# Thirty-two experts as a fixed pipeline on TensorE, with the 32-row experts in 256 columns

## The chip, the cores and the metric

One core of a Trainium2 chip (trn2) runs the whole program. The metric is device time in microseconds of one execution. Before the change it is 2638.91 us, the median of three runs (2637.82 to 2639.2).

## The reference, cut to what matters

The program computes two transformer blocks on 512 tokens of width 1024. Only the last part matters here: the mixture of experts at the end of the second block, and the final norm.

```python
def hierarchical_moe(h, w_rg, b_rg, w_re, b_re, w1, w3, w2):
    ...
    comb = g_w[:, None] * top_p / jnp.sum(top_p, axis=-1, keepdims=True)
    expert = g_idx[:, None] * EXPERTS_PER_GROUP + top_i.astype(jnp.int32)
    ...
    def run_block(args):
        x_blk, e = args
        return (jax.nn.silu(x_blk @ w1[e]) * (x_blk @ w3[e])) @ w2[e]
    ...
    yb = yb * buf_w[:, None].astype(yb.dtype)
    out = jnp.zeros((n_tok + 1, d), yb.dtype).at[buf_tok].add(yb)[:n_tok]
```

Each token goes to two of 32 experts. An expert has two first matrices (w1 and w3, 1024 x 512 each) and a second one (w2, 512 x 1024), all float32: 6 MB in all. The rows that the experts return are weighted, added to their tokens, and the sum is normalised.

## The kernel before, in words

The expert stage is `phase_d`. A router sorts the experts by the number of their tokens; the expert of rank r gets `CAPS[r]` rows: 64, 128 (two experts) or 32 (the last twelve). `GROUPS` puts them into groups of 128 rows (two experts of 64, four of 32, one of 128), and `SEQ` is the order of the 32 experts through the groups: two groups of 64-row experts, four 32-row experts, a 128-row one, two groups of 64, four of 32, a 128-row one, five groups of 64, and four 32-row experts at the end. A few tokens beyond the capacities would go through a loop behind the stage.

Weights come in loads of 1024 KB from SP's queue (`Experts.steps`, L1743): four tiles `w31` per expert (each two of the eight steps of the contraction, w3 and w1 side by side) and two tiles `w2`. All share 18 buffers, three experts' worth, in three pools; a load is issued when a buffer has been read for the last time.

For one group, `begin` selects the group's rows on VectorE (`select`, L1784, into the single buffer `f_sel`), TensorE gathers the rows and turns them (`rows`, L1793), VectorE scales them into `f_X` (L1847), and small products give each row's weight (L1856). For one expert, `hidden` makes the first products: for 64 rows (L1894), p3 and p1 stand in the two halves of one PSUM bank, so that each product uses half the columns of the array and two run beside each other; for 32 rows (L1880), four parts of 128 columns stand beside each other in the array, in two banks. SiLU on ScalarE and a product on VectorE follow (L1896, L1897; L1883, L1884), then `turn_hidden` transposes on TensorE (L1905), ScalarE copies (L66), and `project` makes the second products (L1936; for 32 rows `project_half`, L1918), which `K.split` takes from PSUM into a high and a low half, ScalarE first (L71) and VectorE second (L72). When a group is done, `turned` transposes its selection (L1868), and `scatter` adds the group's rows to the tokens in eight steps (two products each, L1944, and an addition on VectorE, L1946). `last_rows` and `finish` do the last expert, the last scatter, the norm and the stores.

The order on each engine is not that of the text: a planner takes what is ready by its own costs. `issue_after` keeps scatter, turned selection and the next group's rows behind the first products of the current expert; everything else mixes.

Of the kernel before, what the change touches and what calls it, by code (L numbers as in the profile page):

```python
# [10 lines left out]
F32 = mybir.dt.float32  # L11
# [5 lines left out]
AF = mybir.ActivationFunctionType  # L17
OP = mybir.AluOpType
# [1729 lines left out]
def phase_d(K, out):  # L1748
# [3 lines left out]
    with ExitStack() as st:  # L1752
# [90 lines left out]
        def gather(n, sel, combs, room):  # L1843

            X = wk.tile([128, 8, 128], F32, name="f_X", bufs=1)
            for hf, ps in enumerate(room):
                V.tensor_tensor(X[:, 4 * hf:4 * hf + 4, :n], ps[:, :, :n],  # L1847
                                gc[:, 4 * hf:4 * hf + 4, None].to_broadcast([128, 4, n]), op=OP.mult)
            c = wk.tile([128, 4], F32, name="f_c")
            pt = tps.tile([128, 4, 128], F32, name="f_t")  # L1850
            m = n // len(combs)
            top = 128 if m == 32 else m
            for i, w in enumerate(combs):
                for p in range(0, top, m):
# [14 lines left out]
            K.copy(selT[:n], pt[:n], 1)  # L1869
            return selT  # L1870

        def hidden(ts, M, X, c):
            g = wk.tile([128, 512], F32, name="f_g", bufs=1)
            if M == 32:
                p3, p1 = [hps.tile([128, 512], F32, name="f_hp")[:, 0:128] for _ in range(2)]
                for k in range(8):
                    for w, p in enumerate((p3, p1)):
                        for j in range(4):
                            c0 = k % 2 * 1024 + w * 512 + j * 128
                            last = PE.matmul(p[32 * j:32 * j + 32], X[:, k], ts["w31", k // 2][:, c0:c0 + 128],  # L1880
                                             start=k == 0, stop=k == 7, skip_group_check=True,
                                             tile_position=(0, 32 * j))
                S.activation(g[:, 0:128], p1, AF.Silu)  # L1883
                V.scalar_tensor_tensor(g[:, 0:128], p3, c, g[:, 0:128], op0=OP.mult, op1=OP.mult)  # L1884
                return g, last
            if M == 64:
                ps = hps.tile([128, 512], F32, name="f_hp")
                p3, p1 = ps[0:64], ps[64:128]
            else:
                p3, p1 = [hps.tile([128, 512], F32, name="f_hp")[:] for _ in range(2)]  # L1890
            for k in range(8):
                for w, p in enumerate((p3, p1)):
                    c0 = k % 2 * 1024 + w * 512
                    last = PE.matmul(p, X[:, k], ts["w31", k // 2][:, c0:c0 + 512], start=k == 0, stop=k == 7,  # L1894
                                     skip_group_check=True)
            S.activation(g[:M], p1, AF.Silu)  # L1896
            V.scalar_tensor_tensor(g[:M], p3, c[:M], g[:M], op0=OP.mult, op1=OP.mult)  # L1897
            return g, last

        def turn_hidden(M, h):  # L1900

            pg = tps.tile([128, 4, 128], F32, name="f_t")
            n, m = (1, 128) if M == 32 else (4, M)
            for q in range(n):
                PE.transpose(pg[:, q, :m], h[:m, q * 128:(q + 1) * 128], K.ident[:m, :m])  # L1905
            gT = wk.tile([128, 4, 128], F32, name="f_gT", bufs=1)
            K.copy(gT[:, :n, :m], pg[:, :n, :m], 1)
            if M == 32:
                return [gT[:, 0, 32 * q:32 * q + 32] for q in range(4)]
            return [gT[:, q, :M] for q in range(4)]  # L1910

        def project_half(ts, gT, y, a, hf):

            ps = [xps.tile([128, 512], F32, name="f_xp") if hf else yps.tile([128, 512], F32, name="f_yp") for _ in range(2)]
            for k in range(4):
                for j in range(4):
                    c0 = k * 512 + j * 128
                    PE.matmul(ps[j % 2][32 * j:32 * j + 32, 0:128], gT[k], ts["w2", hf][:, c0:c0 + 128],  # L1918
                              start=k == 0, stop=k == 3, skip_group_check=True, tile_position=(0, 32 * j))
            for j in range(4):  # L1920
                cs = slice(128 * j, 128 * j + 128)
                K.split(ps[j % 2][32 * j:32 * j + 32, 0:128], y[0][a:a + 32, hf, cs], y[1][a:a + 32, hf, cs])

        def project(ts, M, gT, y, a):

            if M == 32:
                for hf in range(2):
                    project_half(ts, gT, y, a, hf)
# [19 lines left out]
        def scatter(n, selT, y):  # L1948
            for b in range(NB):
                for hf in range(2):  # L1950
                    add_rows(n, selT, y, b, hf, (yps if hf else xps).tile([128, 512], F32, name="f_yp" if hf else "f_xp"))

        def last_rows(ts, gT, selT, y, a):

# [25 lines left out]
        def finish(parts):  # L1980
# [16 lines left out]
            for b in range(NB):  # L1997
                y = ys[b // 2][:, b % 2]
                V.scalar_tensor_tensor(y, K.x[:, b], rstd[:, b:b + 1], gf, op0=OP.mult, op1=OP.mult)  # L1999
                nc.sync.dma_start(out[b * 128:(b + 1) * 128, :], y)  # L2000

        nxt = begin(0)
        n = 0
        done = None
        for g, rs in enumerate(GROUPS):
            X, sel, c = nxt
            y = None
            for i, r in enumerate(rs):
                M = CAPS[r]
                if n < len(loaded):  # L2010
                    ts = loaded[n]
                elif n < NFIX:
                    ts = W.load(r)
                else:
                    ts = W.load(regs[r])
                    index(n + AHEAD)
                if n == NFIX - 1:
                    for q in range(NFIX, NFIX + AHEAD):
                        index(q)
                h, last = hidden(ts, M, X[:, :, M * i:M * i + M], c[:, i:i + 1])  # L2020
                if n == 0:
                    R.ranks(order, byrank)
                    R.thirds(ranked, byrank[:, 1])
                if i == 0:
                    with tc.issue_after(last.ins):
                        if done:
                            scatter(*done)
                        selT = turned(128, sel)
                if i == len(rs) - 1 and g + 1 < len(GROUPS):
                    with tc.issue_after(last.ins):  # L2030
                        nxt = begin(g + 1)
                gT = turn_hidden(M, h)
                if i == 0:
                    y = halves()
                if n < 31:
                    project(ts, M, gT, y, M * i)
                if n == NFIX:
                    with tc.issue_after(last.ins):
                        R.tables(tab, nov, tabd)
                n += 1  # L2040
            done = 128, selT, y
        finish(last_rows(ts, gT, selT, y, M * i))

        n_over = nc.values_load(nov[0:1, 0:1], min_val=0, max_val=NOV)  # L2044
        nc.sync.dma_start(rankd[:], byrank[:].rearrange("p a b r -> p (a b) r"))
        with tc.For_i(0, n_over, 1) as i:  # L2046
# [16 lines left out]
            project(ts, 64, turn_hidden(64, hidden(ts, 64, X[:, :, :64], c[:, 0:1])[0]), y, 0)  # L2063
            scatter(64, turned(64, sel), y)
            finish(iter(()))


# [315 lines left out]
```

## Time and profile before

| | |
|---|---|
| median of three runs | 2638.91 us |
| the profiled execution | 2639.42 us, span 2637.6 us |
| TensorE products, share of the span | 2491.0 us, 94% |
| VectorE, ScalarE | 1784.1 us (68%), 919.6 us (35%) |
| expert stage | first product at 2136.35 us, last second product ends at 2613.41 us |
| weights of the experts | 192 loads of 1024 KB |

The shares are averages over stages with different limits. The stage before the experts is not touched, so only the last 500 us are read. PE is TensorE, DVE is VectorE, ACT is ScalarE, SPq is the queue of SP. One float32 product is two records on PE. A time in brackets after a row is idle time of the engine before it, with what ended it.

### The profile page before, as it was taken

How to read it: one execution, taken by the hardware profiler on the slowest of the kernel's cores; microseconds unless marked ns; L12 is line 12 of the kernel's file. 1: busy time of each engine (PE TensorE's matmuls, PEld its weight loads, DVE VectorE, ACT ScalarE, POOL GpSimd, SP SyncE). 2: the span in 40 equal slices, each digit the busy share in tenths (PEclk: the TensorE clock that was granted, in tenths of full speed). 3: DMA queues.
4: the chain of work that ended last, by engine and by line, in shares of the span. 5: the costliest groups of instructions: out<-in, count | busy, mean ns of one | idle time of the engine just before them, and what ended most of it. 6: DMA issues, size and time to landing. Idle time of an engine off the chain costs nothing. (4 is left out here: it accounts for less than half of the span.)

```text
span 2637.6 us, 43720 instructions
## 1 busy us (share of the span) xinstructions
PE 2491.0 (94%) x17112; PEld 2075.5 (79%) x17112; DVE 1784.1 (68%) x3778; ACT 919.6 (35%) x1607; POOL 379.6 (14%) x261
## 2 busy tenths in 40 slices
PE   6999999999879999999999998999999989989995
PEld 5887988998869999999998787888797856565554
DVE  6654789988847777878888997576753673333334
ACT  4532533455533333333333344343532412121112
POOL 0000000000004555545555420000000000000000
PEclk8999999999989999999999998898999999999998
DMA  6237122338868999998998973222133489999995
GB/s 244 73 115 241 57 92 81 112 118 253 244 237 300 328 323 322 330 325 314 328 327 322 353 269 117 80 81 72 62 115 116 179 328 401 409 404 386 400 390 213
DMA packets 183483, 623.92 MB, mean 237 GB/s; under 512 B 15846, under 2 KB 66406, under 8 KB 156650
## 3 DMA queue, kind: packets, MB, share of 16 engines
q1 hardware_dynamic: 146410, 486.87, 49.6%
q0 software_dynamic: 36864, 134.23, 14.6%
q8 instruction: 135, 2.21, 0.3%
q14 instruction: 74, 0.61, 0.1%
HBM read 591.55 MB, written 29.49 MB: 235 GB/s over the span
## 5 line engine op out<-in xcount | busy, mean ns | idle before, releaser
L72 DVE TENSOR_TENSOR w_lo<-w_raw,w_hi 128x1024 fp32r<-128x1024 f32 x228 | 278.2, 1220 | 250.1 <-ACT w_hi L71 247.0
L71 ACT CAST w_hi<-w_raw 128x1024 fp32r<-128x1024 f32 x228 | 238.5, 1046 | 579.5 <-issue 205.6
L78 PE MATMUL b_ups<-hT,w_lo 128*128 128x384 f32 x1024 | 347.3, 339 | 6.7 <-DVE w_lo L72 6.5
L76 PE MATMUL b_ups<-hT,w_hi 128*128 128x384 f32 x1024 | 349.6, 341 | 1.4 <-ACT x_sb L919 1.0
L77 PE MATMUL b_ups<-hT,w_hi 128*128 128x384 f32 x1024 | 346.2, 338 | 0.0
L942 POOL DMA_INDIRECT x_sb<-in_u_rows,b_eg x128 | 191.9, 1499 | 979.9 <-ACT b_wh L71 741.2
L76 PE MATMUL b_acc<-b_vh,b_wh 128*128 128x512 f32 x756 | 295.7, 392 | 17.7 <-ACT b_vh L71 17.7
L77 PE MATMUL b_acc<-b_vl,b_wh 128*128 128x512 f32 x756 | 296.7, 392 | 2.9 <-DVE b_vl L72 2.7
L78 PE MATMUL b_acc<-b_vh,b_wl 128*128 128x512 f32 x756 | 295.9, 391 | 0.0
L76 PE MATMUL p_acc<-w_hi,hT 128*128 128x256 f32 x896 | 256.4, 286 | 3.0 <-ACT hT L71 2.8
L77 PE MATMUL p_acc<-w_lo,hT 128*128 128x256 f32 x896 | 253.5, 283 | 1.4 <-DVE w_lo L72 1.3
L78 PE MATMUL p_acc<-w_hi,hT 128*128 128x256 f32 x896 | 253.1, 283 | 0.3 <-DVE hT L72 0.3
L942 POOL DMA_INDIRECT x_sb<-in_v,b_eg x128 | 187.4, 1464 | 199.6 <-DVE b_accg L959 167.0
L78 PEld LDWEIGHTS b_ups<-hT,w_lo 128*128 128x128 f32 x1024 | 194.2, 190 | 9.0 <-DVE w_lo L72 8.9
L76 PEld LDWEIGHTS b_ups<-hT,w_hi 128*128 128x128 f32 x1024 | 194.6, 190 | 6.6 <-ACT b_a L919 1.7
L77 PEld LDWEIGHTS b_ups<-hT,w_hi 128*128 128x128 f32 x1024 | 194.3, 190 | 3.0
L76 PEld LDWEIGHTS p_acc<-w_hi,hT 128*128 128x128 f32 x896 | 171.3, 191 | 18.8 <-issue 13.2
L76 PEld LDWEIGHTS b_acc<-b_vh,b_wh 128*128 128x128 f32 x756 | 142.8, 189 | 44.9 <-ACT b_vh L71 17.9
L77 PEld LDWEIGHTS p_acc<-w_lo,hT 128*128 128x128 f32 x896 | 172.0, 192 | 2.2 <-DVE w_lo L72 1.8
L1894 PE MATMUL f_hp<-f_w,f_X 128*64 128x512 f32 (+1 forms) x640 | 171.4, 594 | 0.7 <-DVE f_X L1847 0.6
L78 PEld LDWEIGHTS p_acc<-w_hi,hT 128*128 128x128 f32 x896 | 170.7, 191 | 1.4 <-DVE hT L72 0.8
L71 ACT CAST b_wh<-b_wfull 128x384 fp32r<-128x384 f32 x128 | 65.4, 514 | 298.8 <-PE b_acc L77 276.4
(660 smaller groups left out, 4916.2 us busy)
## 6 DMA issues: line engine op xcount, KB each, us to landing
f_w<-in_w SPq DMA_DIRECT2D x192, 1024.0 KB
w_raw<-in_u SPq DMA_DIRECT2D x128, 512.0 KB
b_vraw<-in_v SPq DMA_DIRECT2D x128, 512.0 KB
b_gd<-g_sg SPq DMA_DIRECT2D x12, 2048.0 KB
b_g<-b_gd SPq DMA_DIRECT2D x32, 768.0 KB
a_ar_t<-in_w_ada SPq DMA_DIRECT2D x32, 512.0 KB
w_raw<-in_w_tok SPq DMA_DIRECT2D x20, 512.0 KB
a_ar_t<-in_w_ada SPq DMA_DIRECT2D x8, 1024.0 KB
```

The lines of the kernel that those rows point to most:

```text
L71: self.nc.scalar.copy(hi, src)
L72: self.nc.vector.tensor_tensor(lo, src, hi, op=OP.subtract)
L76: first = mm(ps, a[0], b[0], start=start, stop=False)
L77: mm(ps, a[0], b[1], start=False, stop=False)
L78: mm(ps, a[1], b[0], start=False, stop=stop)
L942: nc.gpsimd.indirect_dma_start(out=r, out_offset=None, in_=d[src], in_offset=bass.IndirectOffsetOnAxis(ap=eg[:, k:k + 1], axis=0))
L1894: last = PE.matmul(p, X[:, k], ts["w31", k // 2][:, c0:c0 + 512], start=k == 0, stop=k == 7, skip_group_check=True)
```

## The change

`hidden` gets a function `between` that is called after each of the first seven steps of the contraction. `plan` fills it: in the first expert of a group of several it holds the transposes of the expert before; in the second also the scatter of the former group, two steps at a time, and the turned selection; a group's only expert takes all of it, with the former expert's second products. After an expert's first products (and, for the last expert of a group, the rows of the next group) come the second products of the expert before. A context `in_order` fixes TensorE's order to the order of the text for the whole loop; the `issue_after` blocks go. The 32-row experts have 256 columns per part in place of 128: one PSUM bank for the first products, one for the second, half the instructions, two transposes in place of one. For 128 rows one of the two PSUM banks of the first products comes from the pool `f_xp`.

```diff
-            top = 128 if m == 32 else m
+            top = max(m, 64)
...
-        def hidden(ts, M, X, c):
+        def hidden(ts, M, X, c, between=None):
+
             g = wk.tile([128, 512], F32, name="f_g", bufs=1)
+            ps = hps.tile([128, 512], F32, name="f_hp")
             if M == 32:
-                p3, p1 = [hps.tile([128, 512], F32, name="f_hp")[:, 0:128] for _ in range(2)]
-                for k in range(8):
...
+                n, m = 64, 256
             else:
-                p3, p1 = [hps.tile([128, 512], F32, name="f_hp")[:] for _ in range(2)]
+                n, m = M, 512
+            if M == 128:
+                parts = [(ps, 0, 0, None), (xps.tile([128, 512], F32, name="f_xp"), 1, 0, None)]
+                p3, p1 = parts[0][0][:], parts[1][0][:]
+            else:
+                p3, p1 = ps[0:64, :m], ps[64:128, :m]
+                parts = [(p3, 0, 0, None), (p1, 1, 0, None)]
+                if M == 32:
+                    parts = [(ps[q:q + 32, :m], q // 64, q % 64 // 32 * m, (0, q)) for q in range(0, 128, 32)]
             for k in range(8):
...
+                if between and k < 7:
+                    between(k)
...
-            n, m = (1, 128) if M == 32 else (4, M)
+            n, m = (2, 64) if M == 32 else (4, M)
...
-        def project_half(ts, gT, y, a, hf):
...
+            if M == 32:
+                ps = yps.tile([128, 512], F32, name="f_yp")
+                for k in range(4):
+                    for j in range(4):
+                        c0 = k * 512 + j % 2 * 256
+                        PE.matmul(ps[32 * j:32 * j + 32, 0:256], gT[k], ts["w2", j // 2][:, c0:c0 + 256],
+                                  start=k == 0, stop=k == 3, skip_group_check=True, tile_position=(0, 32 * j))
                 for j in range(4):
...
+                    cs = slice(j % 2 * 256, j % 2 * 256 + 256)
+                    K.split(ps[32 * j:32 * j + 32, 0:256], y[0][a:a + 32, j // 2, cs], y[1][a:a + 32, j // 2, cs])
...
+        def plan(rw, M, first, second, sel):
+
+            p = {}
+            at = lambda k, *f: p.setdefault(k, []).extend(f)
+            if first and second:
+                at(0, rw.turn)
+                at(1, rw.project, lambda: rw.leave())
+                for k in (3, 4, 5, 6):
+                    at(k, rw.scatter_two)
+                at(6, lambda: rw.turned(sel))
+            else:
+                at(3 if M == 64 else 4, rw.turn)
+                if second:
+                    for k in ((2, 3, 4, 5) if M == 64 else (4, 5, 6, 6)):
+                        at(k, rw.scatter_two)
+                    at(5 if M == 64 else 6, lambda: rw.turned(sel))
+            return lambda k: [f() for f in p.get(k, ())]
...
+        with in_order(tc, ("PE",)):
+            for g, rs in enumerate(GROUPS):
...
+                    alone = len(rs) == 1
+                    h = hidden(ts, M, X[:, :, M * i:M * i + M], c[:, i:i + 1], plan(rw, M, i == 0, i == 1 or alone, sel))
...
+                    if i == len(rs) - 1 and g + 1 < len(GROUPS):
                         nxt = begin(g + 1)
...
+                    if not alone:
+                        rw.project()
+                        if i == 0:
+                            rw.leave()
+                    rw.before = ts, M, M * i, h
```

## Rows read from the trace of the kernel before

**Rows 1.** DMA view, 2140 to 2600 us: all transfers of the stretch.

```profile
DMA packets 25156, 183.32 MB, mean 399 GB/s; under 512 B 2783, under 2 KB 2783, under 8 KB 2845
```

**Rows 2.** Busy time by stretch: us of each engine, then clock, DMA share, GB/s.

```profile
2140.00:2200.00 60.00, 59.48 (x518) 30.95 (x518) 35.21 (x80) 10.97 (x19) 0.00 (x0) 1.00 0.96 387
2200.00:2275.00 75.00, 66.53 (x930) 45.49 (x924) 26.65 (x66) 13.83 (x46) 0.00 (x0) 0.98 1.01 418
2275.00:2337.00 62.00, 61.12 (x436) 35.63 (x432) 21.28 (x40) 8.53 (x16) 0.00 (x0) 1.00 0.98 398
...
2413.00:2578.00 165.00, 162.69 (x1054) 88.37 (x1056) 56.27 (x102) 24.45 (x46) 0.00 (x0) 1.00 0.96 386
2578.00:2602.00 24.00, 19.04 (x507) 16.76 (x503) 11.49 (x28) 6.64 (x23) 0.00 (x0) 1.00 0.95 384
```

**Rows 3.** Waits of SP and TensorE in the expert stage: us, times, longest.

```profile
SPq L1743 <- PE f_yp L1936: 176.5, 26, 15.2
SPq L1743 <- PE f_hp L1894: 78.0, 63, 14.5
...
PEld f_hp L1894 <- DMA f_w<-in_w: 0.5, 2, 0.2
```

**Rows 4.** TensorE in order of time, one group of two 64-row experts: start, us.

```profile
2512.76 7.04 PE L1894 MATMUL f_hp<-f_w,f_X 128*64 128x512 f32 x32
2519.72 0.73 PE L1944 MATMUL f_xp<-f_y,f_selT 128*128 128x512 f32 x2
...
2522.13 0.40 PE L1868 MATMUL f_t<-f_id,f_sel 128*128 128x128 f16 x4
...
2524.92 3.94 PE L1936 MATMUL f_yp<-f_w,f_gT 128*64 128x512 f32 x14
...
2536.52 3.75 PE L1793 MATMUL f_xp<-f_sel,f_hs 128*128 128x128 f16 x64
...
2540.55 0.46 PE L1905 MATMUL f_t<-f_ident,f_g 64*128 64x64 f32 x4
2541.52 3.65 PE L1936 MATMUL f_yp<-f_w,f_gT 128*64 128x512 f32 x16 [0.52 <-ACT f_gT L66]
2545.01 1.46 PE L1894 MATMUL f_hp<-f_w,f_X 128*64 128x512 f32 x6
```

**Rows 5.** TensorE in order of time: one first product, two scatter steps, first products.

```profile
2175.95 1.07 PE L1894 MATMUL f_hp<-f_w,f_X 128*64 128x512 f32 x2
2176.95 0.74 PE L1944 MATMUL f_xp<-f_y,f_selT 128*128 128x512 f32 x2
...
2178.10 1.08 PE L1894 MATMUL f_hp<-f_w,f_X 128*64 128x512 f32 x4
```

**Rows 6.** TensorE in order of time, 32-row experts, second and last group of four.

```profile
2337.42 3.70 PE L1880 MATMUL f_hp<-f_w,f_X 128*32 128x128 f32 x128
...
2361.34 1.58 PE L1880 MATMUL f_hp<-f_w,f_X 128*32 128x128 f32 x49 [2.51 <-issue]
...
2381.18 14.00 PE L1894 MATMUL f_hp<-f_w,f_X 128*128 128x512 f32 x32
...
2601.05 1.94 PE L1880 MATMUL f_hp<-f_w,f_X 128*32 128x128 f32 x59 [2.99 <-issue]
...
2611.45 1.08 PE L1918 MATMUL f_yp<-f_w,f_gT 128*32 128x128 f32 x32 [0.41 <-ACT f_gT L66]
2612.35 1.06 PE L1918 MATMUL f_xp<-f_w,f_gT 128*32 128x128 f32 x32
```

**Rows 7.** VectorE in order of time, the same 64-row group: selections and product.

```profile
2525.94 0.75 DVE L1784 TENSOR_TENSOR f_sel<-f_cd,f_byrank 128x256 f16<-128x256 f32 x2
...
2537.25 0.74 DVE L1897 SCALAR_TENSOR_TENSOR f_g<-f_hp,f_c,f_g 64x512 f32<-64x512 f32 x1 [6.19 <-ACT f_g L1896]
```

**Rows 8.** Groups by line and shape: VectorE, low halves of 32-row second products.

```profile
L72 DVE TENSOR_TENSOR f_y<-f_xp,f_y 32x128 fp32r<-32x128 f32 x48 | 13.8, 287 | 3.5 <-ACT f_y L71 2.0
```

More of the change, by code (lines that the diff above doesn't have):

```diff
@@ L1870, in turned @@
             return selT
-        def hidden(ts, M, X, c):
+        def hidden(ts, M, X, c, between=None):
             g = wk.tile([128, 512], F32, name="f_g", bufs=1)
+            ps = hps.tile([128, 512], F32, name="f_hp")
             if M == 32:
-                p3, p1 = [hps.tile([128, 512], F32, name="f_hp")[:, 0:128] for _ in range(2)]
-                for k in range(8):
[L1877 to L1888, printed above, removed]
-            else:
-                p3, p1 = [hps.tile([128, 512], F32, name="f_hp")[:] for _ in range(2)]
-            for k in range(8):
[L1892 to L1898, printed above, removed]
@@ new lines, in hidden @@
+            for k in range(8):
+                for p, w, c0, at in parts:
+                    c0 += k % 2 * 1024 + w * 512
+                    PE.matmul(p if M < 128 else p[:], X[:, k], ts["w31", k // 2][:, c0:c0 + m], start=k == 0, stop=k == 7,
+                              skip_group_check=True, **({"tile_position": at} if at else {}))
+                if between and k < 7:
+                    between(k)
+            S.activation(g[:n, :m], p1, AF.Silu)
+            V.scalar_tensor_tensor(g[:n, :m], p3, c[:n], g[:n, :m], op0=OP.mult, op1=OP.mult)
@@ L1900, in turn_hidden @@
+            return g
         def turn_hidden(M, h):
             pg = tps.tile([128, 4, 128], F32, name="f_t")
-            n, m = (1, 128) if M == 32 else (4, M)
+            n, m = (2, 64) if M == 32 else (4, M)
             for q in range(n):
@@ L1908, in turn_hidden @@
             if M == 32:
-                return [gT[:, 0, 32 * q:32 * q + 32] for q in range(4)]
+                return [gT[:, q % 2, q // 2 * 32:q // 2 * 32 + 32] for q in range(4)]
             return [gT[:, q, :M] for q in range(4)]
-        def project_half(ts, gT, y, a, hf):
[L1914 to L1922, printed above, removed]
         def project(ts, M, gT, y, a):
             if M == 32:
-                for hf in range(2):
-                    project_half(ts, gT, y, a, hf)
+                ps = yps.tile([128, 512], F32, name="f_yp")
[4 more added lines that the diff above has]
+                                  start=k == 0, stop=k == 3, skip_group_check=True, tile_position=(0, 32 * j))
+                for j in range(4):
+                    cs = slice(j % 2 * 256, j % 2 * 256 + 256)
+                    K.split(ps[32 * j:32 * j + 32, 0:256], y[0][a:a + 32, j // 2, cs], y[1][a:a + 32, j // 2, cs])
                 return
@@ L1946, in add_rows, with scattering @@
             V.tensor_tensor(x, x, ps[:], op=OP.add)
-        def scatter(n, selT, y):
+        def scattering(n, selT, y):
             for b in range(NB):
@@ L1951, in scatter @@
                     add_rows(n, selT, y, b, hf, (yps if hf else xps).tile([128, 512], F32, name="f_yp" if hf else "f_xp"))
+                    yield
         def last_rows(ts, gT, selT, y, a):
@@ L2000, in finish, with turn, project, scatter_two @@
                 nc.sync.dma_start(out[b * 128:(b + 1) * 128, :], y)
+        class Rows:
+            before = None
+            scatter = None
+            selT = y = done = None
+            def turn(self):
+                if self.before:
+                    self.gT = turn_hidden(self.before[1], self.before[3])
+            def project(self):
+                if self.before:
+                    ts, M, a, _ = self.before
+                    if not a:
+                        self.y = halves()
+                    project(ts, M, self.gT, self.y, a)
+            def scatter_two(self):
+                if self.scatter:
+                    for _ in range(2):
+                        next(self.scatter, None)
+            def turned(self, sel):
+                self.selT = turned(128, sel)
@@ L2002, in phase_d, with leave @@
+        rw = Rows()
+        def leave():
+            rw.scatter = scattering(128, rw.selT, rw.y) if rw.y else None
+        rw.leave = leave
         nxt = begin(0)
         n = 0
[L2004 to L2030, printed above, removed]
-                        nxt = begin(g + 1)
[L2032 to L2038, printed above, removed]
@@ new lines, in phase_d @@
+        with in_order(tc, ("PE",)):
+            for g, rs in enumerate(GROUPS):
+                X, sel, c = nxt
+                for i, r in enumerate(rs):
+                    M = CAPS[r]
+                    if n < len(loaded):
+                        ts = loaded[n]
+                    elif n < NFIX:
+                        ts = W.load(r)
+                    else:
+                        ts = W.load(regs[r])
+                        index(n + AHEAD)
+                    if n == NFIX - 1:
+                        for q in range(NFIX, NFIX + AHEAD):
+                            index(q)
+                    alone = len(rs) == 1
+                    h = hidden(ts, M, X[:, :, M * i:M * i + M], c[:, i:i + 1], plan(rw, M, i == 0, i == 1 or alone, sel))
+                    if n == 0:
+                        R.ranks(order, byrank)
+                        R.thirds(ranked, byrank[:, 1])
+                    if i == len(rs) - 1 and g + 1 < len(GROUPS):
+                        nxt = begin(g + 1)
+                    if not alone:
[3 more added lines that the diff above has]
+                    rw.before = ts, M, M * i, h
+                    if n == NFIX:
@@ L2039, in phase_d @@
                         R.tables(tab, nov, tabd)
-                n += 1
-            done = 128, selT, y
-        finish(last_rows(ts, gT, selT, y, M * i))
+                    n += 1
+        ts, M, a, h = rw.before
+        gT, y, selT = turn_hidden(M, h), rw.y, rw.selT
+        finish(last_rows(ts, gT, selT, y, a))
         n_over = nc.values_load(nov[0:1, 0:1], min_val=0, max_val=NOV)
@@ L2062, in phase_d @@
             y = halves()
-            project(ts, 64, turn_hidden(64, hidden(ts, 64, X[:, :, :64], c[:, 0:1])[0]), y, 0)
-            scatter(64, turned(64, sel), y)
+            project(ts, 64, turn_hidden(64, hidden(ts, 64, X[:, :, :64], c[:, 0:1])), y, 0)
+            for _ in scattering(64, turned(64, sel), y):
+                pass
             finish(iter(()))
```

## The prediction

> **What bounds the kernel now.** I read the profile from the whole to the single product. The change touches only the expert stage, from the first product at 2136 us to the end at 2637.6 us. I cut that stage into stretches and looked at the DMA column first [rows 2]: the transfers move 384 to 418 GB/s in every stretch, while TensorE's busy column is nearly full too. Two resources are close to their limit, so the next question is which one waits for the other.
>
> The stage's weight transfers say how far the DMA side is from full. From 2140 to 2600 us 183.3 MB move at a mean of 399 GB/s [rows 1]; the best long stretch, 2200 to 2275, holds 418 GB/s with a share of 1.01 [rows 2]. I take 418 as full. Against it the stretches lost: 2140 to 2200, 60 x (1 - 387/418) = 4.4 us; 2275 to 2337, 62 x (1 - 398/418) = 3.0 us; 2413 to 2578, 165 x (1 - 386/418) = 12.6 us. That is 20.0 us in which transfers had nothing to do. The last stretch, 24 us at 384, holds 22.0 us of full rate, so the last weights land near 2600.
>
> The waits name the cause [rows 3]: SP, which issues the loads, waits 176.5 us for second products (L1936) and 78.0 us for first products (L1894) to free a buffer, while TensorE waits for a load 0.5 us in all. So TensorE is the pacer where the queue runs dry, and the queue where it does not.
>
> A group of two 64-row experts shows the pacer [rows 4]: 2512.76 to 2545.01, 32.25 us. One load of 1024 KB at 418 GB/s takes 2.51 us, six per expert, so two experts need 30.1 us of transfer: 2.15 us of dry queue per group, and five such groups (10.8 us) make most of the 12.6. Four 32-row experts are the reverse [rows 6]: TensorE is through in 43.8 us (2337.42 to 2381.18), their loads need 60.2 us, and the buffers filled ahead are used up.
>
> **The change, part by part.** *64-row group on TensorE.* Its pieces today, start to start [rows 4]: first products 6.96 us; second products 3.49; rows and weights of the next group 4.03 (2536.52 to 2540.55); transposes 0.46; the turned selection 0.40. The second stretch of products, 2524.92 to 2536.52, takes 11.60 where 6.96 + 3.49 = 10.45 would do, because products of two experts are mixed there; with the gap of 0.52 us before 2541.52 and the slow end of the scatter that is what a fixed order can give back. New: the scatter goes in four pairs between first products. An interrupted pair took 1.15 us (2176.95 to 2178.10) [rows 5], five uninterrupted steps (2519.72 to 2522.13, four of the five rows left out) 2.41 us, or 0.96 a pair [rows 4]. I take 1.15, since the new pairs are interrupted. Sum: 2 x 6.96 + 2 x 3.49 + 4.03 + 2 x 0.46 + 0.40 + 4 x 1.15 = 30.85 us, 1.40 less than now and still 0.75 above the transfers' 30.1. With 0.96 it is 30.1.
>
> *The waits on the way.* The transposes now stand four steps (3.5 us) after the former expert's products end; SiLU and the product on VectorE must fit in, and 0.74 us for the latter [rows 7] leaves room. The new wait to watch is the selection: its buffer is single, it is read until the turned selection after step five, and the next group's rows follow after two more steps, 2 x 0.87 = 1.74 us. Behind it on VectorE stand two scatter additions; two selections took 0.75 us in all [rows 7]. That fits if they run before the product of the expert just finished, as today (2525.94 against 2537.25). If they come behind it, the rows wait for SiLU, product and selections: the product ended at 2537.99, 1.47 us after the first products gave way to the rows at 2536.52 [rows 4, 7], and 0.75 comes on top, 2.2 us per group; TensorE's whole order is then held, since it is fixed. I take 0, with 2.2 as the upper end.
>
> *32-row experts.* Twice the columns, half the instructions, same streamed columns: the 3.70 us of one expert's first products [rows 6] stay. The exposed chain before each expert's transpose and second products, and the unexplained gaps of 2.51 and 2.99 us [rows 6], go or shrink; one transpose becomes two (0.46 / 4 = 0.12 us more). Evacuation: eight parts of 287 ns become four [rows 8], bounded by 4 x 287 and 4 x 574 ns, off the path. TensorE gains about 10 us per group of four, but the 60.2 us of loads set this stretch: worth nothing by itself. What it does is keep the buffers emptier when the 64-row groups begin.
>
> *128-row experts* lose the pause in which nothing but scatter ran; loads bind there, I count nothing. Halved weight products beside the rows: hidden by the same pacing.
>
> *Late release.* The second weights of an expert are now freed after the next expert's first products (6.96 us later) and, for the first of a pair, after the next rows too (4.03 us). Loads behind them on SP's list wait along. At the start, where every buffer is full and TensorE paces, this costs between 0 and 11 us of dry queue; I take 8, near the upper end, since nothing is buffered against it. Later the queue is behind anyway and it costs nothing; if TensorE became slower again, each group would pay there too.
>
> **The sum.** Dry queue: 4.4 + 8 stay at the start; 3.0 and 12.6 go, because TensorE reaches the late groups about 10 us earlier than the refill that today fills the ring, and 0.75 us x 5 groups does not use that up. Last load: 2600 - (20.0 - 12.4) = 2592.4. Today the last second product ends 13.4 us later, at 2613.41 [rows 6], because TensorE lags; with TensorE waiting for the queue only that product is left, 2612.35 + 1.06 - 2611.45 = 2.0 us [rows 6]. So 2594.4 instead of 2613.4, 19.0 us. The tail of 24.2 us behind it is unchanged. The profiled execution took 2639.42 us, 0.5 above the median; 2639.4 - 19.0 = 2620.4, against the median 2620.
>
> **Two rules against the change.** The row says that the queue sustained 418 GB/s for 75 us [rows 2]. The Trainium skill, page "DMA: Bandwidth & Descriptors", section Specifications, gives about 358 GB/s as what the memory serves one core: the stage's 183.3 MB would then need 512 us, more than the 460 it took, and nothing could be gained. The measurement decides against that figure. And breaks are not free: an unpaired 64-row product cost 1.00 us (2175.95 to 2176.95) [rows 5] where it costs 0.44 in a row of pairs (6.96 / 16). The Trainium skill, page "TensorEngine Tiling (Array Packing)", Key Properties, says that changing the tiling mode drains TensorE; this change adds such switches, and the third rival below is what it would do.
>
> **Rivals.** *TensorE stays the pacer.* Waits of 1 to 2 us per group (the selection, a PSUM buffer) leave 32 us per group; only the last 32-row group and the lag at the end are gained, about 6 to 10 us: 2629 to 2633. For: the order can no longer fill a hole. *The queue is the limit already.* If 399 GB/s is what this traffic really reaches and the dry spots are its grain, loads end where they end, and the lag is partly re-made: 2636 to 2642. Against: SP's 254 us of waits for products. *Broken pairs, slower.* Six breaks per 64-row group; if each leaves one product unpaired, 6 x 0.56 = 3.4 us, the group takes 34.2 us, 2.0 more than now, over eight steady groups 16 us, less some 9 us at the end: +7, 2646. It decides from about 0.4 us per break on (0.2 already eats the group's gain). For: the 1.00 us row; against: breaks here fall on whole pairs of products, and the measured interrupted pair of steps was only 0.19 us dearer.
>
> **Chances.** What can be told from no change here is about 0.2%, 5.3 us. The forecast, 2607 to 2629, gets 0.60; TensorE as pacer 0.14; the queue as limit 0.10; broken pairs or the late selection at every group 0.16. So faster 0.74, same 0.10, slower 0.16. Lower end: no dry queue at all, 20.0 + 11.4 us = 31.4, 2607.5, rounded down to 2606. Upper end 2641, through the case of no change, which leaves out the slower one.
>
> **What would show it.** Right: a 64-row group near 31 us; 410 GB/s or more from the first 32-row group to the last load; waits of TensorE for f_w of several us near the ends of the 32-row groups; the last second product about 2 us behind the last load; no gap over 1 us among 32-row products. Wrong: a wait of rows (L1793) for f_sel in every group, single products of 1.00 us beside scatter steps, SP still waiting for second products in the late groups, or a stage before 2136 us that moved.

## The result, and the profile after

The changed kernel takes 2622.46 us (median of 11 runs, 2616.69 to 2633.74) beside 2636.66 us for the kernel before (11 runs, 2631.25 to 2646.87): a ratio of 0.9946, 95% interval 0.9931 to 0.9962, that is 10 to 18 us less. Run a second time among the experiments it came to 0.9931 (0.9913 to 0.9948). The forecast was 2620 us, a ratio of 0.9928 to the median that it started from. One run of the reordered loads below fell in a slow state, at 6226.33 us, and is left out of every figure.

The profiled execution took 2626.2 us, span 2624.4. Busy time by stretch, columns as in [rows 2], the first stretch from 2136 us:

```profile
2136.00:2200.00 64.00, 62.62 (x490) 32.37 (x491) 41.39 (x114) 9.81 (x18) 0.00 (x0) 0.96 0.78 312
2200.00:2275.00 75.00, 70.04 (x602) 36.62 (x601) 25.98 (x51) 12.48 (x31) 0.00 (x0) 0.93 1.01 421
2275.00:2337.00 62.00, 62.00 (x456) 28.65 (x454) 23.01 (x42) 9.48 (x18) 0.00 (x0) 1.00 1.01 419
2337.00:2413.00 76.00, 69.23 (x594) 35.96 (x592) 25.52 (x51) 12.70 (x31) 0.00 (x0) 0.93 1.01 420
2413.00:2578.00 165.00, 165.00 (x1196) 77.46 (x1196) 65.44 (x116) 26.87 (x52) 0.00 (x0) 1.00 1.01 416
```

From 2200 us to the last load the queue now moves 416 to 421 GB/s without a hole; the 398 and 386 of before are gone. The price stands in the first line: 312 GB/s, where the kernel before moved 365 over the same 64 us (314 and 366 when each is counted from the start of its own expert stage):

```profile
2136.00:2200.00 64.00, 63.13 (x538) 32.88 (x542) 38.62 (x102) 10.97 (x19) 0.00 (x0) 1.00 0.91 365
```

The waits of SP and TensorE in the expert stage, as in [rows 3]:

```profile
SPq L1743 <- DMA f_w<-in_w: 195.6, 108, 3.4
SPq L1743 <- PE f_yp L1930: 115.3, 18, 18.2
...
SPq L1743 <- PE f_hp L1891: 22.8, 10, 14.5
...
PE f_hp L1891 <- DMA f_w<-in_w: 14.7, 10, 4.6
...
PE f_xp L1793 <- DVE f_sel L1784: 1.5, 1, 1.5
```

SP's waits for products have fallen from 254.5 to 138.1 us, and TensorE now waits for loads, 14.7 us. The rows wait for the selection once, at the start, and in no group behind. One group of two 64-row experts on TensorE, in order of time, as in [rows 4]:

```profile
2433.21 3.63 PE L1891 MATMUL f_hp<-f_w,f_X 128*64 128x512 f32 x16
2436.77 0.46 PE L1904 MATMUL f_t<-f_ident,f_g 64*128 64x64 f32 x4
...
2440.64 3.60 PE L1930 MATMUL f_yp<-f_w,f_gT 128*64 128x512 f32 x16
2444.08 2.74 PE L1891 MATMUL f_hp<-f_w,f_X 128*64 128x512 f32 x12
2446.75 0.73 PE L1938 MATMUL f_xp<-f_y,f_selT 128*128 128x512 f32 x2
2447.32 0.63 PE L1938 MATMUL f_yp<-f_y,f_selT 128*128 128x512 f32 x2
2447.88 1.08 PE L1891 MATMUL f_hp<-f_w,f_X 128*64 128x512 f32 x4
2448.89 0.46 PE L1904 MATMUL f_t<-f_ident,f_g 64*128 64x64 f32 x4
...
2456.80 3.75 PE L1793 MATMUL f_xp<-f_sel,f_hs 128*128 128x128 f16 x64
...
2464.18 1.06 PE L1891 MATMUL f_hp<-f_w,f_X 128*64 128x512 f32 x4
```

2433.21 to 2464.18 is 30.97 us, without a gap. An interrupted pair of scatter steps takes 1.13 us (2446.75 to 2447.88), and the step of products behind it 1.01 in place of 0.87. On VectorE the selection and the product of the same group, as in [rows 7]:

```profile
2455.53 0.76 DVE L1784 TENSOR_TENSOR f_sel<-f_cd,f_byrank 128x256 f16<-128x256 f32 x2
2457.54 0.74 DVE L1896 SCALAR_TENSOR_TENSOR f_g<-f_hp,f_c,f_g 64x512 f32<-64x512 f32 x1 [1.26 <-ACT f_g L1895]
```

The selection comes first and is done half a microsecond ahead of the rows at 2456.80. At the end of the first group of 32-row experts TensorE stands three times, as in [rows 6] but with another releaser:

```profile
2222.06 1.07 PE L1891 MATMUL f_hp<-f_w,f_X 128*32 128x256 f32 x16 [2.42 <-DMA f_w<-in_w]
2224.45 1.94 PE L1891 MATMUL f_hp<-f_w,f_X 128*32 128x256 f32 x16 [1.32 <-DMA f_w<-in_w]
2226.93 1.08 PE L1891 MATMUL f_hp<-f_w,f_X 128*32 128x256 f32 x8 [0.55 <-DMA f_w<-in_w]
```

The gaps without a releaser are gone; the loads are what it waits for.

Whole executions are hard to compare, for the untouched part ahead of the experts ends at a different time in each: the first group's second half of rows (32 products of `rows`) begins at 2132.43 us before and 2137.03 after, and between 2127.88 and 2137.47 in the kernels below. So I also compare the **stage**, from there to the end of the last scatter step, in the one profiled execution of each; the changed kernel's two gave 469.4 and 468.6 us. The table is worked out from the traces' start and end times:

```
kernel                                    from      to        stage us
before                                    2132.43   2618.70   486.3
before, five loads                        2129.53   2608.87   479.3
before, 256 columns                       2137.47   2608.72   471.2
changed                                   2137.03   2606.45   469.4
changed, second execution                 2132.31   2600.94   468.6
changed, 128 columns                      2134.63   2603.31   468.7
changed, scatter in one block             2134.35   2603.03   468.7
changed, early second products            2127.88   2592.78   464.9
changed, loads reordered                  2131.12   2589.20   458.1
the same, second execution                2131.74   2592.16   460.4
reordered, last products by halves        2133.19   2593.89   460.7
reordered, scatter in one block           2133.12   2594.53   461.4
changed, five loads                       2130.59   2571.76   441.2
changed, five loads, scatter in one block 2130.05   2566.37   436.3
```

### The profile page after: what moved, and what is told of

Same layout as the page of the kernel before. It is cut to its first block, busy times and chain, and to the rows that moved or that the text cites. A ratio compares the mean times of both kernels' runs of the same rounds, so it can differ in the third digit from the quotient of the medians.

```text
span 2624.4 us, 41077 instructions
## 1 busy us (share of the span) xinstructions
PE 2492.6 (95%) x15876; PEld 2018.9 (77%) x15876; DVE 1782.3 (68%) x3730; ACT 913.2 (35%) x1559; POOL 376.8 (14%) x261
## 5 line engine op out<-in xcount | busy, mean ns | idle before, releaser
L1891 PE MATMUL f_hp<-f_w,f_X 128*32 128x256 f32 (+2 forms) x1376 | 212.4, 508 | 15.6 <-DMA f_w<-in_w 14.7
L959 DVE SCALAR_TENSOR_TENSOR b_accg<-x_sb,b_ag,b_accg 128x1024 f32<-128x1024 f32 x127 | 162.9, 1283 | 11.6 <-DMA x_sb<-in_v,b_eg 10.4
```

The lines of the kernel that those rows point to most:

```text
L959: tc.keep_in_program_order(V.scalar_tensor_tensor(accg[:], r, ag[:, k:k + 1], accg[:], op0=OP.mult, op1=OP.add))
L1891: PE.matmul(p if M < 128 else p[:], X[:, k], ts["w31", k // 2][:, c0:c0 + m], start=k == 0, stop=k == 7, skip_group_check=True, **({"tile_ ...
```

## The experiments

All were timed in five rounds beside the kernel before. The question of the first four: which part of the change gained, what the late release of the second weights costs, and what is the bound now.

**The pipeline alone.** The changed kernel with the 32-row experts as before:

```diff
-            n, m = (2, 64) if M == 32 else (4, M)
+            n, m = (1, 128) if M == 32 else (4, M)
...
-                ps = yps.tile([128, 512], F32, name="f_yp")
...
+                for hf in range(2):
+                    project_half(ts, gT, y, a, hf)
```

> The changed kernel with the 32-row experts back in parts of 128 columns (second products in one PSUM bank per half), so the pipeline alone. Theory (weights' queue paces the stage once TensorE's order has no holes, and the 32-row stretches are paced by the queue anyway): the ratio to before stays within 0.002 of the changed kernel's 0.9946, that is 0.993 to 0.997. Rival (half the instructions of the 32-row experts make the gain): most of the gain goes, 0.998 or more.

Measured: 2621.84 us beside 2639.33, ratio 0.9942 (0.9921 to 0.9964); stage 468.7 us. The pipeline alone gives the whole gain, as far as the interval can tell.

**The 256 columns alone.** The kernel before with the 32-row experts of the changed one:

```diff
-                p3, p1 = [hps.tile([128, 512], F32, name="f_hp")[:, 0:128] for _ in range(2)]
+                ps = hps.tile([128, 512], F32, name="f_hp")
...
-                for hf in range(2):
-                    project_half(ts, gT, y, a, hf)
+                ps = yps.tile([128, 512], F32, name="f_yp")
```

> The kernel before with the 32-row experts in 256 columns and nothing else, so the other part alone. Theory: TensorE still paces the 64-row groups at 32.2 us and the late stretch still runs at about 386 GB/s; at most the last group's lag shrinks, 0 to 4 us, ratio 0.9985 to 1.000. Rival (the wide columns make the gain): 10 us or more, 0.996 or less.

Measured: 2629.08 us, ratio 0.9957 (0.9943 to 0.9972), 7 to 15 us less; stage 471.2, 15.1 less. My theory fell, and with it a step of the prediction: this part, too, gives most of the gain by itself. The two gains don't add. Busy time by stretch, this kernel:

```profile
2275.00:2337.00 62.00, 61.40 (x406) 35.59 (x402) 21.95 (x41) 8.58 (x17) 0.00 (x0) 1.00 1.01 420
...
2413.00:2578.00 165.00, 162.66 (x1069) 90.37 (x1065) 60.10 (x109) 24.56 (x46) 0.00 (x0) 1.00 0.99 406
```

406 GB/s in place of 386 [rows 2], though a 64-row group still takes 32.24 us here. TensorE came out of the second group of 32-row experts earlier: from the rows at 2330.27 to those at 2432.27 it needed 102.0 us, where the kernel before needed 111.6 (2328.23 to 2439.79). That lead stood in free buffers, which the next groups let fill again: twelve loads in 32.24 us are 390 GB/s, and 406 were moved. Where the time went shows in TensorE's waits of the kernel before:

```profile
PE f_hp L1880 <- issue: 8.4, 5, 3.0
...
PE f_xp L1793 <- issue: 1.9, 1, 1.9
...
PE f_yp L1918 <- issue: 1.4, 2, 0.8
PE f_xp L1918 <- issue: 1.2, 1, 1.2
```

These are 12.9 us in which TensorE stood among the 32-row experts with no releaser in the profile. With half the instructions there is no such wait at all, and 12.9 of the 15.1 us are accounted for.

**Second products early in the first two groups.** After the changed kernel's first two groups the buffers of their first experts' second weights come free sooner:

```diff
+                    if early:
+                        at(early, rw.project)
...
-                    if not alone:
+                    if not alone and n not in (1, 3):
                         rw.project()
```

> The changed kernel with the second products of the first expert of groups 0 and 1 moved forward, from behind the next group's rows into the first products of the second expert (behind step 5 and 6). It frees two weight tiles 5 to 6 us earlier at the start. Theory (every microsecond of dry queue at the start reaches the end, because the queue is never dry afterwards): 3 to 7 us less than the changed kernel, 2616 to 2619 on a scale where that has 2622.5. Rival (TensorE paces the late groups, so the start is made up or lost there): no change, or 3 us more, since TensorE now waits for the next group's rows to be scaled.

Measured: 2617.14 us, ratio 0.9923 (0.9909 to 0.9937); the changed kernel was not run in this batch, and its 0.9946 of another is 6 us more; stage 464.9, 4 us less. As the theory had it: the queue is less dry at the start. This execution entered its stage 4.4 us earlier than the changed kernel's second one, so I count 64 us from four microseconds behind the start of the stage:

```profile
2131.88:2195.88 64.00, 62.86 (x480) 29.94 (x484) 37.37 (x99) 10.44 (x19) 0.00 (x0) 1.00 0.84 341
```

The changed kernel moved 313 GB/s there (its line stands with the late release below). With 420 as the full rate that is 4.3 us less of dry queue, though TensorE pays for the earlier place (its second 64-row group took 32.24 us again, 2151.18 to 2183.42).

**Five loads in place of six.** The changed kernel with less for the queue to do:

```diff
-        for n, m in (("w31", 4), ("w2", 2)):
+        for n, m in (("w31", 4), ("w2", 2 if isinstance(e, int) else 1)):
...
+                if (n, m) == ("w2", 1):
+                    ts[n, 1] = t
```

> The changed kernel with five loads in place of six for each of the last 28 experts; their second w2 tile is left out and the first is read twice (so half of each second product uses the wrong matrix), with TensorE's work unchanged. Theory (queue is the bound, TensorE close behind): TensorE becomes the pacer of the 64-row groups at about 31 us and its waits for loads, some 15 us in the 32-row stretches, go: 10 to 18 us less than the changed kernel, not the 70 us that the 28 loads took. Rival (TensorE paces already): less than 4 us.

Measured: 2594.71 us, ratio 0.9833 (0.982 to 0.9846), 30 us below the changed kernel; stage 441.2, 27 to 28 us less. The direction is that of the theory, the size is far over it. The queue sets the changed kernel's time; TensorE alone would need 27 to 28 us less. TensorE waits for no load here, and the late stretch shows a queue with time to spare:

```profile
2413.00:2578.00 165.00, 156.62 (x1232) 74.95 (x1228) 69.25 (x134) 35.16 (x79) 0.00 (x0) 0.98 0.75 302
```

The expectation counted TensorE's waits for loads alone, 14.7 us in the changed kernel. The rest of the difference is in its busy time over the whole stage, here of the changed kernel and of the one with five loads:

```profile
2137.03:2606.45 469.42, 450.74 (x3536) 221.45 (x3535) 190.99 (x389) 80.63 (x176) 0.00 (x0) 0.96 0.96 395
2130.59:2571.76 441.17, 437.17 (x3536) 219.22 (x3535) 190.98 (x389) 80.58 (x176) 0.00 (x0) 0.99 0.86 353
```

The same 3536 product records took 450.7 us and 437.2. Behind the waits at the end of the first 32-row group the granted clock was 0.50 (2224.4 to 2231.3 us), the lower of its two levels, 1.2 GHz, and 16 records took 1.94 us in place of 1.07; with five loads it was 1.00 from 2200 to 2413 us. In the second execution of the changed kernel the waits were 18.9 us and the busy time 445.8, and the stage was as long, which fits a stage whose end the queue sets.

**The kernel before with five loads.** Since the 256 columns alone gained, the question was whether the queue had set any stretch of the kernel before. The edit is the same as above.

> The kernel before, with five loads in place of six for each of the last 28 experts: the second tile of second weights is left out and the first one is used twice, so the output is another. 28 loads, 70 us of queue time, are taken away. Theory (TensorE, not the queue, sets the pace of the kernel before in every stretch, the 32-row experts among them, since it never waits for a load there): the time hardly moves, 0 to 4 us less, ratio 0.9985 to 1.000. Rival, and my prediction (the loads of four 32-row experts, 60.2 us against 43.8 us on TensorE, set that stretch): 10 us less of loads in each of two 32-row groups and in the last, 12 to 25 us, ratio 0.990 to 0.995.

Measured: 2633.68 us beside 2642.26, ratio 0.9973 (0.9954 to 0.9991), 2 to 12 us less; stage 479.3, 7.0 less. It lies between the two expectations, nearer to the theory: 70 us of queue time are worth 7. Its waits of TensorE:

```profile
PE f_hp L1883 <- issue: 6.4, 3, 2.5
...
PE f_xp L1921 <- issue: 1.2, 1, 1.2
PE f_xp L1796 <- issue: 0.5, 1, 0.5
```

8.1 us without a releaser in place of 12.9: 4.8 of the 7.0 us are these gaps again. A 64-row group took 32.10 us for 32.24, 1.1 us over eight groups. The kernel before waited 0.5 us for weights in all [rows 3]: its pace was TensorE's. Fewer loads shortened gaps whose cause is not shown.

**Loads in the order in which buffers come free.** The changed kernel reads the first weights of expert n+1 before the second weights of expert n, but loads them the other way round, so loads stand behind one whose buffer is freed later. A generator `order` replaces `steps`:

```diff
+        for q in range(33):
+            for n, m, k in (("w31", 4, q), ("w2", 2, q - 1)):
+                if not 0 <= k < 32:
+                    continue
...
-                        ts = W.load(regs[r])
+                    for _ in range(issued, 6 * n + 4):
+                        next(loads)
```

> The changed kernel with its loads put in the order in which their buffers are read and freed: the first weights of the next expert before the second weights of the former, so that no load stands in line behind one whose buffer is freed later. Theory (the late release of the second weights is what empties the queue at the start, about 16 us of dry queue between 2136 and 2200 us, and after 2200 us the queue sets the pace): the stretch from 2136 to 2200 us rises from 312 to over 350 GB/s, the last load and the end come 5 to 9 us earlier than in the changed kernel, ratio 0.991 to 0.9925. Rival (the queue is dry there because all buffers are full while TensorE works off the first experts, whatever the order): within 2 us of the changed kernel, ratio 0.9935 or more.

With it ran the changed kernel once more:

> The changed kernel once more, as the reference for the three kernels run beside it. Both theories: as measured, a ratio of 0.993 to 0.996, some 12 to 18 us less than before.

Measured: 2616.13 us (five runs) beside 2640.28, ratio 0.991 (0.989 to 0.9929); the changed kernel 2622.04, ratio 0.9931. That is 5.9 us less, though the intervals overlap; stage 458.1 and, in a second run, 460.4, for 468.6. In a later batch the ratio was 0.992 (0.9898 to 0.9942). Busy time by stretch, loads reordered, the first line from four microseconds behind the start of the stage:

```profile
2135.12:2199.12 64.00, 64.00 (x504) 30.89 (x508) 38.12 (x101) 11.33 (x20) 0.00 (x0) 1.00 0.93 378
2200.00:2275.00 75.00, 73.44 (x596) 38.67 (x594) 29.41 (x57) 12.50 (x31) 0.00 (x0) 1.00 1.01 420
```

378 GB/s for 313: of 64 us, 6.4 are dry (1 - 378/420) where 16.3 were. The 9.9 us between them are the 8 to 10 us of the stage. The late release was the cause, as predicted, and an order of loads undoes it at no cost to TensorE.

**Scatter in one block.** The changed kernel with four breaks fewer in a 64-row group:

```diff
-                    for k in ((2, 3, 4, 5) if M == 64 else (4, 5, 6, 6)):
+                    for k in ((5, 5, 5, 5) if M == 64 else (4, 5, 6, 6)):
```

> The changed kernel with the eight scatter steps of a 64-row group in one block behind step five in place of four pairs between products: four breaks fewer a group. Theory (queue sets the pace from 2200 us on): a group at the queue's 30 to 31 us whatever TensorE saves, the time within 3 us of the changed kernel. Rival (TensorE, at 30.97 us a group, still sets the pace of the 64-row groups): the change of the group's length times eight groups is seen in the time, 0.5 us a group less being 4 us less in all; a block that waits for VectorE's additions would cost as much.

> The changed kernel with five loads in place of six, as before, and the scatter of a 64-row group in one block: here TensorE sets the pace, so that the breaks show their price. Theory (a pair of scatter steps that breaks into products costs 0.15 to 0.3 us more, with the step behind it): a 64-row group falls from 30.97 to between 30.0 and 30.7 us, the time 2 to 8 us below the pipeline with five loads (ratio 0.9833). Rival (a block of eight steps runs into VectorE's additions of 0.68 us each, with four PSUM buffers): a group of 31 us or more, no gain or a loss.

Measured in the changed kernel: 2620.62 us, ratio 0.9919 (0.9902 to 0.9937), not to be told from 0.9931, and the stage is the same, 468.7. With five loads, where TensorE is the bound: 2587.95 us, ratio 0.9807 (0.9782 to 0.9832) for 0.9833, and stage 436.3 for 441.2. The rows for the next group in the kernel with five loads, of two groups that follow one another:

```profile
2428.06 3.73 PE L1796 MATMUL f_xp<-f_sel,f_hs 128*128 128x128 f16 x64 [0.22 <-DVE f_sel L1787]
...
2458.46 3.73 PE L1796 MATMUL f_xp<-f_sel,f_hs 128*128 128x128 f16 x64 [0.22 <-DVE f_sel L1787]
```

30.40 us a group for 30.97, a new wait of 0.22 us for the selection included: four breaks cost 0.57 to 0.79 us, 0.14 to 0.20 each. In the changed kernel the groups shrank as much and the time didn't: the late stretch moved 419 GB/s for 416, and what TensorE saves in the groups it loses among the last four experts (59.2 us from the last group's rows to the last scatter step, 56.7 and 55.2 in the two executions without the edit).

**Two edits on top of the reordered loads** gained nothing that can be told. The last expert's second products by halves:

```diff
+            half(0)
             for hf in range(2):
                 for b in range(NB):
+                    if hf == 0 and b == 2:
+                        half(1)
```

> The kernel with the reordered loads and, for the last expert, second products by halves: the first half, its evacuation and two of its additions of rows stand ahead of the second half, whose weights land last. Theory (behind the last load stand second products, their evacuation and the scatter, in series, on the path that sets the end): 1.5 to 3 us less than the kernel with the reordered loads, and the time from the last load's landing to the last addition of rows falls by as much. Rival (the end waits for VectorE's additions of rows and the norm, not for TensorE): within 1 us of it.

Measured: 2614.56 us, ratio 0.99 (0.9882 to 0.9919) beside 0.991. The median is 1.6 us lower, at the edge of the theory's range, but the intervals overlap widely and the stage is not shorter, 460.7 beside 458.1 and 460.4: this stays open. In the trace the last weights were there before TensorE reached them, and the two halves took longer than the one piece (TensorE in order of time):

```profile
2581.56 1.92 PE L1973 MATMUL f_yp<-f_w,f_gT 128*32 128x256 f32 x16 [0.75 <-ACT f_gT L66]
...
2586.47 3.60 PE L1973 MATMUL f_xp<-f_w,f_gT 128*32 128x256 f32 x16
```

The second half ran at a mean granted clock of 0.59 (2586.0 to 2590.2), most of it at the lower of the two levels, behind waits for the evacuation; with the 1.92 us of the first the stage would by estimate have been 459.0, that of the reordered kernel.

> Reordered loads and the scatter of a 64-row group in one block, the two edits that gained, together. Theory (with the reordered loads the queue hardly waits any more, so TensorE at 30.97 us a group sets the pace of the last 64-row groups again, and the block's 30.4 us a group is worth its difference there): 2 to 5 us less than the kernel with reordered loads alone, ratio 0.9885 to 0.9905. Rival (the queue is the bound to the last load, as in the changed kernel): within 1.5 us of it, ratio 0.9905 to 0.9915.

> The kernel with the reordered loads once more, as the reference beside the one with both edits: ratio 0.990 to 0.992 as measured.

Scatter in one block on top: 2613.79 us beside 2636.1, ratio 0.9911 (0.9889 to 0.9932), with 0.992 for the reordered loads alone in the same batch; stage 461.4 beside 460.4. The groups shrank to 30.40 us again and TensorE's waits for loads grew from 11.7 to 15.8 us, so the trace speaks for the rival. No version with all six loads can be told to be faster than the reordered loads alone, 19 to 29 us below the kernel before in the first batch and 15 to 27 in the second.

## Why the prediction was right, and where not

- **Time and sign.** 2620 forecast, 2622.46 measured, inside the range; the gain was 10 to 18 us in one comparison and 14 to 23 in the other, for 19.0 forecast. (The lower end of the range, 2607.5 rounded down, is 2607 and not 2606; nothing hangs on it.)
- **The end of the stage.** Forecast: last load near 2592.4, last second product 2594.4. The second execution of the changed kernel began its stage at the time of before (2132.31 for 2132.43). Its last second products on TensorE:

```profile
2590.88 0.63 PE L1918 MATMUL f_yp<-f_w,f_gT 128*32 128x256 f32 x4 [0.50 <-ACT f_gT L66]
2592.30 1.92 PE L1918 MATMUL f_yp<-f_w,f_gT 128*32 128x256 f32 x28 [0.80 <-DMA f_w<-in_w]
2595.53 0.95 PE L1938 MATMUL f_hp<-f_y,f_selT 128*128 128x512 f32 x2 [1.31 <-ACT f_y L71]
```

  The wait for the load ended at 2592.30, the product at 2594.22. The tail behind it was 25.3 us (to 2619.5) in place of the 24.2 taken as unchanged: the scatter now waits 1.31 us for evacuations of 256 columns. The profiled execution of the first comparison did the same 4.6 us later, because it entered the stage 4.6 us later.
- **The full rate.** 418 GB/s was taken as full from one stretch; the changed kernel holds 416 to 421 for nearly 380 us. The sum left out the stretch from 2337 to 2413 us, 414 GB/s before, which is 0.7 us. What the Trainium skill, page "DMA: Bandwidth & Descriptors", section Specifications, gives for one core's memory (358 GB/s) does not hold in these rows; by it there would have been no gain.
- **The 64-row group.** 30.85 us forecast, 30.97 measured; the interrupted pair 1.15 forecast, 1.13 measured. The broken pairs of the third rival cost 0.14 to 0.20 us each, which the forecast's interrupted pairs held already, and not the 0.56 of an unpaired product. The drain that the Trainium skill, page "TensorEngine Tiling (Array Packing)", Key Properties, names for a change of mode agrees in that breaks cost something; the page gives no price, and the runs do. No run tells a drain from other costs of a break.
- **The selection.** Taken as 0; 0 in every later group. It stands ahead of the product of the expert just finished, the order on which the 0 rested.
- **32-row experts: the step that failed.** "The 60.2 us of loads set this stretch: worth nothing by itself." Alone they are worth 15.1 us of the stage. The prediction compared the two engines' work stretch by stretch and gave each stretch to the larger. But its own [rows 3] said that TensorE waited 0.5 us for loads in all: the loads of those stretches came from a stock, and what TensorE gains in one stretch it carries into the next as free buffers. The prediction's sum did count on such a lead ("TensorE reaches the late groups about 10 us earlier"), so this step and the sum don't agree; with the 256 columns alone TensorE reached them 12.6 us earlier, from the start of the stage. The kernel before with five loads says the same from the other side: 28 loads less were worth 7 us.
- **The late release.** 8 us of dry queue taken, in bounds of 0 to 11, on top of 4.4. The kernel before and the changed kernel's second execution, each from four microseconds behind the start of its stage:

```profile
2136.43:2200.43 64.00, 63.48 (x554) 33.23 (x558) 38.19 (x100) 10.97 (x19) 0.00 (x0) 1.00 0.91 366
2136.31:2200.31 64.00, 64.00 (x504) 30.87 (x508) 38.10 (x101) 11.33 (x20) 0.00 (x0) 1.00 0.78 313
```

  With 420 as full, 8.2 and 16.3 of the 64 us are dry: 8.1 more. The size held, but no row had fixed the 8 within its bounds, so that it came so close is partly luck. One load shows the wait: the first of the sixth expert's second weights stood 18.2 us, until the third expert's second products ended at 2195.7 us; before it was 10.0. Behind 2200 us the late release was taken as free. The queue moved 415 and 416 GB/s in the late stretch of the two executions, 1.6 to 2.0 us dry, and a full rate of 420 for 418 over some 390 us gave about as much back.
- **A sign that misleads.** "SP still waiting for second products in the late groups" was to show the prediction wrong. SP did wait, from 2413 to 2578 us:

```profile
SPq L1743 <- PE f_yp L1930: 53.1, 9, 13.9
```

  The queue moved 416 GB/s meanwhile: a wait of SP alone is not a dry queue, and the GB/s decide.
- **The bound behind.** By the stages with five loads TensorE's own work fell from 479.3 to 441.2 us, 38 us; the queue let 17 of them through. The prediction named the queue as the next limit; that TensorE would be 27 to 28 us under it, it did not say.

## What to carry to other kernels

An engine that never waits for its loads is likely the bound everywhere, as here, also in stretches whose loads take longer than its work: the buffers carry a lead from one stretch to the next, so sum both sides over the whole stage and compare the sums. When two edits relieve the same engine and another limit lies close, measure each alone: their gains don't add. If an order of use is changed, change the order of loads with it, so that no load stands behind one whose buffer is freed later.

## What the runs showed of the hardware

- **Gaps without a releaser beside instruction fetches.** The nine gaps of this kind in the kernel before, 12.9 us, each end 1.2 to 1.5 us after the end of a 16 KB transfer of the queue that carries instructions. From 2337 to 2385 us that queue moved (packets, MB, share), in the kernel before and in the one with 256 columns:

```profile
q8 instruction: 7, 0.11, 1.0%
```

```profile
q8 instruction: 4, 0.07, 0.6%
```

  Half the instructions, about half the fetches, no gaps. That TensorE waited for its instructions there is argued from this, not shown: no run changed the fetches alone.
- **The clock of single executions.** In the untouched part, from 2062 to 2070 us, the granted clock was 1.00 in the profiled execution of before and 0.57 in that of the changed kernel:

```profile
2062.00:2070.00 8.00, 7.93 (x46) 6.05 (x47) 3.55 (x7) 2.22 (x3) 0.00 (x0) 1.00 0.83 288
```

```profile
2062.00:2070.00 8.00, 6.58 (x11) 2.91 (x11) 4.36 (x8) 0.59 (x1) 0.00 (x0) 0.57 0.47 158
```

  Between 1.00 (2.4 GHz) and 0.50 (1.2 GHz) such a mean is a mix of the two levels. The kernel with 256 columns alone had 0.58 there and entered its stage 5.0 us late; the changed kernel's second execution had 0.88 and was on time. Whether the clock made them late or both have one cause is not shown. At the end, from 2584 to 2595 us, the two executions of the changed kernel had 0.54 and 1.00, both with TensorE waiting for loads. What tells them apart was not tried.
